# Order of four pieces of work at the edges of the feed-forward products, and the sizes of two down parts

## Chip, cores and metric

The kernel runs on one core of one Trainium2 chip. The metric is the device time of one execution in microseconds (us). Beside it stands one profiled execution, from which all rows below are taken.

## What is computed

The reference applies two layers and then one block to a sequence of 1024 positions of width 1024, all in fp32:

```python
for layer in range(2):
    y = conv_lru_mixer(x, ...) if layer == 0 else diff_attention_mixer(x, ...)
    x = layer_norm(DN_ALPHA * x + y, mix_ln_g[layer], mix_ln_b[layer])
    x = layer_norm(DN_ALPHA * x + swiglu(x, w_gate, w_up, w_down), ffn_ln_g[layer], ffn_ln_b[layer])
...
c_mod = silu(c) @ w_ada + b_ada            # six rows: sh1, sc1, g1, sh2, sc2, g2
...                                        # mLSTM and Fourier mixer of block 2
h2 = ln_plain(x) * (1 + sc2) + sh2
ff = square(relu(h2 @ w_ff1 + b_ff1)) @ w_ff2 + b_ff2
out = ln_affine(ALPHA * x + (1 + g2) * ff, ln2_g, ln2_b)
```

`swiglu(x, g, u, d)` is `(silu(x @ g) * (x @ u)) @ d`, with 2816 inner columns (22 tiles of 128); block 2 has 4096 (32 tiles).

## The kernel before

Every fp32 operand is split into a high part (a copy rounded to the matmul's format, made by ScalarE, L213) and a low part (the difference, made by VectorE, L214). A product then takes three matmuls, high by high (L235), high by low (L236) and low by high (L237). A weight tile arrives in a slot of the pool `raw` (three slots of 4 KB a partition, issued by SyncE at L218) and is split into `wh` and `wl`, or into the pair `wd`.

The sequence stands in 8 token blocks of 128. The three stretches of feed-forward work (layers 0 and 1, block 2) each have two stages.

**Up stage.** `run_ffn` goes over units, each a 2 by 2 block product by Winograd's scheme with seven products instead of eight: `prepare` loads two raw weight tiles, splits A11 and A12, and forms the sums S1 to S4 with four VectorE instructions (L674 to L677). `product` runs seven terms of 12 matmuls (128x128 by 128x512): A11·B11 and A12·B21 on `wx` (`corner`, `corner2`), T2, T3 and T4 on `wy`, T1 and B22 on `wz`. Between them stand small instructions: `keep` (L693, ScalarE) is a copy of A11·B11, `wy += keep` (L707, VectorE), a copy `u` of `wy` (L709, ScalarE), a copy `p` of `wz` (L713), `wz += u` (L714), and the sum for block 22 (L758, inside `sum22`), which must be done before T4 goes on with `wy`. The results are written to memory (`hd`).

The activations' blocks T1 to T3 and the sums of them (`bs`, `bl`) are formed by `xn.sums` on VectorE, once per pair of token blocks. Before the last sums exist, the products of the corner alone can run; `start` issues some of these early units (table `EARLY`) while the mixer before it ends. This overlap of a mixer's last token blocks with the first units is called a front here: one each in layer 0, layer 1 and block 2. The stage tables of `pipe` give the order in which `more` (it calls `start`) and `xn.sums` are issued.

**Down stage.** The inner tiles are cut into parts (`PARTS1`, `PARTS2`), each a number of inner tiles and the pool in which its split weights lie. A part goes over the 8 token blocks; `tokens` loads the activated tiles of a block back (`ht`, L831, in pieces of at most four inner tiles) and splits them, `down_tile` multiplies them (6 matmuls for each inner tile), and `add` adds the result to `xr` (L898). In the last part the token blocks also go through the layer norm and the first products of what follows (`stages`; `pv` are value projections), one behind another. While layer 1 goes through its parts, a side stream loads the 48 tiles of `w_ada` (two per token block), which VectorE multiplies and sums (L1240).

The text is written in program order, but a list scheduler turns it into the order in which each engine runs its instructions; every engine then works strictly in that order, and so does SyncE's queue of transfers.

Of the kernel before, what the change touches and what calls it, by code (L numbers as in the profile page):

```python
# [30 lines left out]
PARTS1 = ((8, "x"), (6, "u"), (4, "x"), (4, "u"))  # L31
# [129 lines left out]
class Net:  # L161
# [248 lines left out]
    def mixer_even(self, xr, xn, start):  # L410
# [220 lines left out]
        for c in range(NC1, 4):  # L631
# [3 lines left out]
                         (LE + ME[2], more), (LE + 1, norm), (LE + 2, feat), (LE + 3, xn.sums), (LE + 3, more)],  # L635
# [64 lines left out]
    def product(self, o, x, keep, finish, sum22, early):  # L700
# [13 lines left out]
        nc.vector.tensor_add(pz, pz, u2)  # L714
        self.term(py, o["S3"], x, "T3", False, True)
        sum22(py, p5)
        if not early:
            self.corner2(o, x, px, finish)
# [5 lines left out]
    def run_ffn(self, nf, x, src, nm, done, parts, down_weight, load, add, stages, side=None, add_half=None):  # L724
# [67 lines left out]
        o = prep(0)  # L792
        while begun:
            finish_first()
        for n, (q, m) in enumerate(order):
            nxt = prep(n + 1) if n + 1 < len(order) else None
            finish, sum22 = finisher(q, m)
            self.product(o, x, keep(q, m), finish, sum22, (q, m) in started)
            if m == nm - 1:
                ctx.pop(q)  # L800
            if n % 2:
                kept.pop(n // 2)
            o = nxt
            steps(SD[n % 2])

# [14 lines left out]

        def tokens(j, i):
            n, hs = parts[j][0], []
            for a in range(0, n, 4):
                e = min(n, a + 4)
                shape = (P, 2, e - a, P)
                if add_half is None and j == len(parts) - 1:
                    t = self.u("ht", shape, F32R)
                else:
                    t = self.wp.tile(list(shape), F32R, tag="w", name=self.name("ht"))
                raw = t[:, 1].bitcast(F32)  # L830
                nc.sync.dma_start(raw, hd[j][a:e, :, blk(i)].rearrange("f p t -> p f t"))  # L831
                self.split(t[:, 0], t[:, 1], raw)
                hs += [(t[:, 0, b, :], t[:, 1, b, :]) for b in range(e - a)]
# [3 lines left out]
        ws, hs = {0: weights(0)}, {}  # L837
# [139 lines left out]
    def mixer_odd(self, x, xr, xn, start):  # L977
# [218 lines left out]
        for _ in last:  # L1196
# [6 lines left out]
                   (LO + MO[1], more), (LO + MO[2], more), (LO + 3, sums), (LO + 3, more)])  # L1203
# [122 lines left out]
    def block2_mix(self, x, xr, xn, start):  # L1326
# [480 lines left out]
        def more(i):  # L1807
            if i == NTT - 1:
# [4 lines left out]
                  + [(LM, feat), (0, moments), (LM + 1, lambda i: xn.sums(i) if i >= 4 else None), (LM + 1, more)])  # L1813

    def block2_ff(self, x, xr, out):
# [15 lines left out]
        def load(i):  # L1831
            if i == 0:
# [3 lines left out]
                nc.gpsimd.tensor_mul(st["b2"], st["b2"], st["g2"])  # L1836
# [3 lines left out]
        def add(i, p, first, last):  # L1840
            nc.vector.scalar_tensor_tensor(xr[i], xr[i], ALPHA2 if first else 1.0, p, op0=ALU.mult, op1=ALU.add,
                                           accum_out=self.sum_of(xr[i]) if last and S4 else None)
            if cnt[i] == 1:
                nc.gpsimd.tensor_add(xr[i], xr[i], st["b2"])
# [180 lines left out]
```

## Time and profile before

| | |
|---|---|
| time, median of 3 runs | 3423.69 us (3421.68 to 3425.16) |
| profiled execution, its own time | 3421.3 us |
| its span | 3419.5 us |
| TensorE (PE) busy | 3269.5 us, 96% of the span |
| VectorE (DVE) busy | 2185.5 us, 64% |
| ScalarE (ACT) busy | 1412.9 us, 41% |
| GpSimd (POOL) busy | 265.6 us, 8% |
| mean granted clock of TensorE | 0.985 of full speed |

The span runs from the first to the last instruction; the execution's own time is 1.8 us longer. A time in the rows counts from the span's start. Matmuls are pipelined, so that one lasts longer than the distance to the next, and what counts for TensorE is the idle time in brackets ahead of an instruction with the instruction that ended it, and the clock that was granted.

### The profile page before, as it was taken

The page shows a single profiled execution, that of the slowest core. Times are in us where ns is not written, and L with a number is a line of the kernel's source. Part 1 is how long each engine was busy: PE and PEld are TensorE (multiplying, and loading weights), DVE is VectorE, ACT ScalarE, POOL GpSimd, SP SyncE. Part 2 cuts the span into 40 slices and gives each one's busy share as a digit, 9 for nine tenths or more (in the row PEclk, how much of TensorE's full clock was granted, in tenths as well). Part 3 has the DMA queues.
Part 4 walks back from the last instruction along what each step waited for, and adds up shares of the span by engine and source line. Part 5 has one row for each costly group of instructions (what it writes and reads, how often), then busy time and mean ns, then how long its engine had stood idle before and what let it go on. Part 6 is the DMA issues. An engine that isn't in the chain of part 4 may idle for free.

```text
span 3419.5 us, 40944 instructions
## 1 busy us (share of the span) xinstructions
PE 3269.5 (96%) x15588; PEld 2692.5 (79%) x15588; DVE 2185.5 (64%) x3445; ACT 1412.9 (41%) x2422; POOL 265.6 (8%) x458
## 2 busy tenths in 40 slices
PE   8998999999999999989999999999999989999998
PEld 7776788878877878877788878778777878878887
DVE  8997755555357677676765558654446876566635
ACT  4455433332237667655533332224334554432211
POOL 1011000000020111101000000013001300000201
PEclk9999999999999999999999999999999999999999
DMA  3131322235312111141332238721123333344312
GB/s 126 42 112 62 101 91 74 91 128 169 106 62 71 36 50 50 43 149 56 109 107 99 93 120 290 237 74 47 59 84 106 116 117 117 116 161 165 113 51 79
DMA packets 191764, 348.68 MB, mean 102 GB/s; under 512 B 14384, under 2 KB 105936, under 8 KB 191568
## 3 DMA queue, kind: packets, MB, share of 16 engines
q1 hardware_dynamic: 191568, 346.07, 30.6%
q8 instruction: 122, 2.00, 0.2%
q14 instruction: 74, 0.61, 0.1%
HBM read 268.41 MB, written 72.36 MB: 100 GB/s over the span
## 4 chain that ended last, share of the span: by engine, by line
PE 66%; DVE 13%; ACT 9%; DMA 5%; issue 4%; POOL 3%; SPq 0%; POOLq 0%; DVEq 0%; ACTq 0%
PE dn L236 6%; PE dn L235 6%; PE dn L237 6%; PE wy L235 4%; PE wy L236 4%; PE wy L237 4%; PE wx L235 3%; PE wx L237 3%; PE wx L236 3%; PE pi L235 3%; PE pi L236 3%; PE pi L237 2%; PE wz L235 2%; PE wz L237 2%; PE wz L236 2%
## 5 line engine op out<-in xcount | busy, mean ns | idle before, releaser
L213 ACT CAST wh<-raw 128x1024 fp32r<-128x1024 f32 (+1 forms) x275 | 282.7, 1048 | 405.1 <-DVE raw L677 138.1
L214 DVE TENSOR_TENSOR wl<-raw,wh 128x1024 fp32r<-128x1024 f32 (+1 forms) x275 | 334.3, 1233 | 132.1 <-ACT wh L213 128.1
L213 ACT CAST ht<-ht 128x512 fp32r<-128x512 f32 (+1 forms) x168 | 97.2, 580 | 448.0 <-DMA ht<-hd 438.7
L235 PE MATMUL dn<-wd,ht 128*128 128x512 f32 x704 | 274.4, 391 | 3.3 <-ACT wd L213 3.3
L236 PE MATMUL dn<-wd,ht 128*128 128x512 f32 x704 | 274.8, 390 | 1.3 <-DVE wd L214 1.2
L237 PE MATMUL dn<-wd,ht 128*128 128x512 f32 x704 | 274.4, 390 | 0.0
L235 PE MATMUL dn<-wh,ht 128*128 128x512 f32 x512 | 200.9, 392 | 10.8 <-DVE xr L898 6.7
L214 DVE TENSOR_TENSOR ht<-ht 128x512 fp32r<-128x512 f32 (+1 forms) x168 | 112.3, 673 | 153.2 <-ACT ht L213 152.4
L235 PE MATMUL wx<-bh,wh 128*128 128x512 f32 x480 | 192.2, 400 | 10.6 <-ACT keep L693 4.2
L237 PE MATMUL wx<-bh,wl 128*128 128x512 f32 x480 | 190.2, 397 | 11.2 <-DVE wl L214 11.2
L237 PE MATMUL dn<-wh,ht 128*128 128x512 f32 x512 | 200.3, 391 | 0.4 <-DVE ht L214 0.4
L236 PE MATMUL dn<-wl,ht 128*128 128x512 f32 x512 | 200.2, 391 | 0.0
L236 PE MATMUL wx<-bl,wh 128*128 128x512 f32 x480 | 190.3, 396 | 0.0
L235 PE MATMUL pi<-xh,wh 128*128 128x512 f32 x416 | 168.8, 406 | 7.8 <-DVE xl L214 7.8
L486 DVE SCALAR_TENSOR_TENSOR co<-ga,col,co 128x512 f32<-128x512 f32 (+18 forms) x240 | 165.4, 737 | 0.5
L237 PE MATMUL pi<-xh,wl 128*128 128x512 f32 x416 | 165.0, 397 | 0.0
L236 PE MATMUL pi<-xl,wh 128*128 128x512 f32 x416 | 164.9, 396 | 0.0
L235 PEld LDWEIGHTS dn<-wd,ht 128*128 128x128 f32 x704 | 132.3, 188 | 32.0 <-ACT wd L213 4.6
L236 PEld LDWEIGHTS dn<-wd,ht 128*128 128x128 f32 x704 | 132.4, 188 | 30.3 <-DVE wd L214 2.9
L237 PEld LDWEIGHTS dn<-wd,ht 128*128 128x128 f32 x704 | 132.4, 188 | 27.5
L287 POOL TENSOR_SCALAR nm<-sum 128x1 f32<-128x1 f32 x47 | 15.1, 322 | 1562.8 <-DVE xr L898 1323.1
L898 DVE SCALAR_TENSOR_TENSOR xr<-xr,dn 128x1024 f32<-128x1024 f32 x64 | 77.8, 1216 | 85.5 <-PE dn L237 81.3
(458 smaller groups left out, 8446.4 us busy)
## 6 DMA issues: line engine op xcount, KB each, us to landing
raw<-w_gu SPq DMA_DIRECT2D x100, 512.0 KB
hd<-g SPq DMA_DIRECT2D x152, 256.0 KB
raw<-w_f SPq DMA_DIRECT2D x70, 512.0 KB
ht<-hd SPq DMA_DIRECT2D x136, 256.0 KB
raw<-w_ada SPq DMA_DIRECT2D x48, 512.0 KB
raw<-w_dn SPq DMA_DIRECT2D x44, 512.0 KB
raw<-w_in SPq DMA_DIRECT2D x26, 512.0 KB
raw<-w_out SPq DMA_DIRECT2D x24, 512.0 KB
```

The source lines that it names most:

```text
L213: self.nc.scalar.copy(hi, src)
L214: (self.nc.gpsimd if pool else self.nc.vector).tensor_sub(lo, src, hi.bitcast(F32))
L235: mm(out, l[0], r[0], start=first, stop=False, **kw)
L236: mm(out, l[0], r[1], start=False, stop=False, **kw)
L237: mm(out, l[1], r[0], start=False, stop=last, **kw)
L287: (nc.vector if NMV else nc.gpsimd).tensor_scalar(nm, a, -1.0 / D, None, op0=ALU.mult)
L486: nc.vector.scalar_tensor_tensor(co[c][:, a:hi_], ga[c][:, a - s:hi_ - s], self.c("conv_w", 31 * c + 30 - s), co[c][:, a:hi_], op0=ALU.mul ...
L898: nc.vector.scalar_tensor_tensor(xr[i], xr[i], DN_ALPHA if first else 1.0, p, op0=ALU.mult, op1=ALU.add, accum_out=self.sum_of(xr[i]) if l ...
```

## The change

1. In layers 0 and 1 the parts of the down product change from 8, 6, 4, 4 inner tiles to 8, 4, 4, 6. The last part, of six, takes its `ht` tiles from the pool `raw` instead of the pool `u`.
2. In `product`, A12·B21 runs ahead of T3 instead of behind it.
3. The weights of the first down part are issued ahead of the last unit's product instead of behind it.
4. At the three fronts the last `more` (early units) is issued ahead of the last `xn.sums`.
5. In block 2 the bias row `b2` is scaled, and added to the 8 token blocks, by VectorE instead of GpSimd.

```diff
--- before.py
+++ after.py
@@ -28,7 +28,7 @@
 NF2 = 4096 // P
 NEG = -1.0e30
 EARLY, WAHEAD = (1, 1, 2, 2), 2
-PARTS1 = ((8, "x"), (6, "u"), (4, "x"), (4, "u"))
+PARTS1 = ((8, "x"), (4, "u"), (4, "x"), (6, "u"))
 PARTS2 = ((8, "x"), (6, "u"), (8, "x"), (6, "u"), (4, "x"))
 L2 = 2
 DV = 1
@@ -632,7 +632,7 @@
             conv(c, 1)
         more = lambda i: start() if i == NTT - 1 else None
         self.pipe(pre + [(0, lambda i: feat(i - 4)), (LE, prod_a), (LE + ME[0], more), (LE + ME[1], more),
-                         (LE + ME[2], more), (LE + 1, norm), (LE + 2, feat), (LE + 3, xn.sums), (LE + 3, more)],
+                         (LE + ME[2], more), (LE + 1, norm), (LE + 2, feat), (LE + 3, more), (LE + 3, xn.sums)],
                   range(4, 8))
 
     def mixer_end(self, xr, xn, layer):
@@ -712,10 +712,10 @@
         p5 = self.tmp("p5")
         nc.scalar.copy(p5, pz)
         nc.vector.tensor_add(pz, pz, u2)
+        if not early:
+            self.corner2(o, x, px, finish)
         self.term(py, o["S3"], x, "T3", False, True)
         sum22(py, p5)
-        if not early:
-            self.corner2(o, x, px, finish)
         self.term(pz, o["S4"], x, "B22", False, True)
         finish(0, 1, pz)
         self.term(py, o["A22"], x, "T4", False, True)
@@ -788,20 +788,6 @@
         def prep(n):
             q, m = order[n]
             return self.prepare(src(2 * q, m), src(2 * q + 1, m), first=(q, m) not in started)
-
-        o = prep(0)
-        while begun:
-            finish_first()
-        for n, (q, m) in enumerate(order):
-            nxt = prep(n + 1) if n + 1 < len(order) else None
-            finish, sum22 = finisher(q, m)
-            self.product(o, x, keep(q, m), finish, sum22, (q, m) in started)
-            if m == nm - 1:
-                ctx.pop(q)
-            if n % 2:
-                kept.pop(n // 2)
-            o = nxt
-            steps(SD[n % 2])
 
         def weights(j):
             n, kind = parts[j]
@@ -818,13 +804,30 @@
                 ws.append((t[:, e, :], t[:, e + 1, :]))
             return ws
 
+        ws = {}
+        o = prep(0)
+        while begun:
+            finish_first()
+        for n, (q, m) in enumerate(order):
+            nxt = prep(n + 1) if n + 1 < len(order) else None
+            finish, sum22 = finisher(q, m)
+            if nxt is None:
+                ws[0] = weights(0)
+            self.product(o, x, keep(q, m), finish, sum22, (q, m) in started)
+            if m == nm - 1:
+                ctx.pop(q)
+            if n % 2:
+                kept.pop(n // 2)
+            o = nxt
+            steps(SD[n % 2])
+
         def tokens(j, i):
             n, hs = parts[j][0], []
             for a in range(0, n, 4):
                 e = min(n, a + 4)
                 shape = (P, 2, e - a, P)
                 if add_half is None and j == len(parts) - 1:
-                    t = self.u("ht", shape, F32R)
+                    t = self.rp.tile(list(shape), F32R, tag="raw", name=self.name("ht"))
                 else:
                     t = self.wp.tile(list(shape), F32R, tag="w", name=self.name("ht"))
                 raw = t[:, 1].bitcast(F32)
@@ -834,7 +837,7 @@
             return hs
 
         todo = [(j, i) for j in range(len(parts)) for i in range(NTT)]
-        ws, hs = {0: weights(0)}, {}
+        hs = {}
 
         def ahead(n):
             if n < len(todo) and todo[n] not in hs:
@@ -1200,7 +1203,7 @@
         more = lambda i: start() if i == NTT - 1 else None
         sums = lambda i: xn.sums(i) if i >= 4 else None
         self.pipe([(0, lambda i: heads4(i, 4)), (LO + MO[0], more), (LO + 2, feat), (LO + 1, norm), (LO, o_prod),
-                   (LO + MO[1], more), (LO + MO[2], more), (LO + 3, sums), (LO + 3, more)])
+                   (LO + MO[1], more), (LO + MO[2], more), (LO + 3, more), (LO + 3, sums)])
 
     def ada(self):
         nc, A = self.nc, self.A
@@ -1810,7 +1813,7 @@
 
         stats = lambda i: self.ln_stats(xr[i])
         self.pipe([(3, stats), (4, stats), (1, prep), (3, norm1), (4, norm2), (2, prod)] + [(m, more) for m in MF]
-                  + [(LM, feat), (0, moments), (LM + 1, lambda i: xn.sums(i) if i >= 4 else None), (LM + 1, more)])
+                  + [(LM, feat), (0, moments), (LM + 1, more), (LM + 1, lambda i: xn.sums(i) if i >= 4 else None)])
 
     def block2_ff(self, x, xr, out):
         nc, A = self.nc, self.A
@@ -1833,7 +1836,7 @@
                 st["b2"] = self.u("b2")
                 r12 = ROWS.index("b_ff2")
                 nc.sync.dma_start(st["b2"], A["rows"][r12:r12 + 1, :].to_broadcast([P, D]))
-                nc.gpsimd.tensor_mul(st["b2"], st["b2"], st["g2"])
+                nc.vector.tensor_mul(st["b2"], st["b2"], st["g2"])
             xr.append(self.u("xr"))
             nc.sync.dma_start(xr[i], self.xs[2][blk(i), :])
 
@@ -1841,7 +1844,7 @@
             nc.vector.scalar_tensor_tensor(xr[i], xr[i], ALPHA2 if first else 1.0, p, op0=ALU.mult, op1=ALU.add,
                                            accum_out=self.sum_of(xr[i]) if last and S4 else None)
             if cnt[i] == 1:
-                nc.gpsimd.tensor_add(xr[i], xr[i], st["b2"])
+                nc.vector.tensor_add(xr[i], xr[i], st["b2"])
             cnt[i] += 1
 
         def add_half(i, p, cs):
```

The numbers of matmuls and their sizes stay. How the order on the engines changes is seen at three places. A line number behind the edit is 3 higher in the changed kernel (L887 is L890, L971 is L974), and the number at the end of a tile's name counts tiles and differs between the two.

**VectorE at the front of layer 0.** `wl_2714` is the low part of the weights of the early unit that TensorE waits for, in the changed kernel `wl_2698`; `ts`, `bs` and `bl` (L150 to L153, L214) are the sums, and the last `bl_2448` closes them. Before:

```order
L153 TENSOR_TENSOR ts_2661<-f_2229,ts_2660 128x512
L887 TENSOR_TENSOR g_2619<-g_2619,wx_2593 128x512
L214 TENSOR_TENSOR bl_2448<-ts_2660,bh_2447 128x8x128
L214 TENSOR_TENSOR bs_2453<-ts_2661,bs_2451 128x2x128
L214 TENSOR_TENSOR bs_2454<-ts_2661,bs_2452 128x2x128
L214 TENSOR_TENSOR bs_2461<-ts_2661,bs_2459 128x2x128
L214 TENSOR_TENSOR bs_2462<-ts_2661,bs_2460 128x2x128
L214 TENSOR_TENSOR wl_2714<-raw_2711,wh_2713 128x1024
L214 TENSOR_TENSOR w_390_2755<-raw_2753,w_390_2755 128x512
L674 TENSOR_TENSOR raw_2753<-raw_2753 128x512
L675 TENSOR_TENSOR raw_2753<-raw_2751,raw_2753 128x512
L676 TENSOR_TENSOR raw_2751<-raw_2753,raw_2751 128x512
```

In the changed kernel `wl` is found among the sums of the pair before the last:

```order
L150 TENSOR_TENSOR ts_2644<-f_2523,f_2154 128x512
L152 TENSOR_TENSOR ts_2645<-f_2523 128x512
L151 TENSOR_TENSOR ts_2644<-f_2523,ts_2644 128x512
L214 TENSOR_TENSOR wl_2698<-raw_2695,wh_2697 128x1024
L214 TENSOR_TENSOR bs_2352<-f_2631,bs_2350 128x2x128
L214 TENSOR_TENSOR bs_2353<-f_2631,bs_2351 128x2x128
L153 TENSOR_TENSOR ts_2645<-f_2154,ts_2644 128x512
L214 TENSOR_TENSOR bl_2448<-ts_2644,bh_2447 128x8x128
```

And the last sums are found some ten rows further on:

```order
L676 TENSOR_TENSOR raw_2751<-raw_2753,raw_2751 128x512
L677 TENSOR_TENSOR raw_2751<-raw_2751 128x512
L150 TENSOR_TENSOR ts_2729<-f_2631,f_2229 128x512
L152 TENSOR_TENSOR ts_2730<-f_2631 128x512
L151 TENSOR_TENSOR ts_2729<-f_2631,ts_2729 128x512
L214 TENSOR_TENSOR wl_2763<-raw_2751,wh_2762 128x1024
L153 TENSOR_TENSOR ts_2730<-f_2229,ts_2729 128x512
L214 TENSOR_TENSOR bl_2448<-ts_2729,bh_2447 128x8x128
L214 TENSOR_TENSOR bs_2453<-ts_2730,bs_2451 128x2x128
L214 TENSOR_TENSOR bs_2454<-ts_2730,bs_2452 128x2x128
```

`wl` moved from behind the sums of the last pair to the middle of the sums of the pair before it, and the sums of the weights (L674 to L677) moved ahead of the last sums, which now end with `bl_2448` behind `wl_2763`.

**VectorE at the last unit of layer 0.** `xr` is the residual's first scaling (L894 and L895, L897 and L898 in the changed kernel), `wd` the weights of the first down part. Before:

```order
L214 TENSOR_TENSOR ht_5375<-ht_5375 128x512
L894 TENSOR_TENSOR xr_5449<-xr_5449,gb_5383 128x1024
L707 TENSOR_TENSOR wy_5242<-wy_5242,keep_5126 128x512
L895 TENSOR_TENSOR xr_5449<-xr_5449,gb_5385 128x1024
L214 TENSOR_TENSOR wd_5333<-raw_5331,wd_5333 128x1024
L714 TENSOR_TENSOR wz_5258<-wz_5258,u_702_5256 128x512
L214 TENSOR_TENSOR wd_5333<-raw_5336,wd_5333 128x1024
L758 TENSOR_TENSOR p_704_5271<-wy_5242,p_704_5271 128x512
L214 TENSOR_TENSOR wd_5342<-raw_5340,wd_5342 128x1024
L887 TENSOR_TENSOR g_5185<-g_5185,p_704_5271 128x512
```

In the changed kernel:

```order
L897 TENSOR_TENSOR xr_5449<-xr_5449,gb_5383 128x1024
L214 TENSOR_TENSOR ht_5375<-ht_5375 128x512
L898 TENSOR_TENSOR xr_5449<-xr_5449,gb_5385 128x1024
L707 TENSOR_TENSOR wy_5278<-wy_5278,keep_5126 128x512
L214 TENSOR_TENSOR wd_5230<-raw_5228,wd_5230 128x1024
L214 TENSOR_TENSOR wd_5230<-raw_5233,wd_5230 128x1024
L214 TENSOR_TENSOR wd_5239<-raw_5237,wd_5239 128x1024
L714 TENSOR_TENSOR wz_5294<-wz_5294,u_714_5292 128x512
L890 TENSOR_TENSOR g_5185<-g_5185,wx_5264 128x512
L758 TENSOR_TENSOR p_716_5307<-wy_5278,p_716_5307 128x512
```

`wy += keep` (L707) moved behind both instructions on `xr_5449`, and three `wd` stand ahead of `wz += u` (L714) instead of one.

**SyncE's queue in the last down part of layer 0.** `ht` are the activated tiles (of the part `hd_95`), `raw<-w_v` the value weights for the `pv` products of layer 1's mixer, `spill` the layer's result written to memory. Before, where `w_v` had been issued long ahead of this part:

```order
L831 DMA ht_6711<-hd_95 128x4x128
L971 DMA spill<-xr_5387 128x1024
L831 DMA ht_6775<-hd_95 128x4x128
L971 DMA spill<-xr_5449 128x1024
L831 DMA ht_6894<-hd_95 128x4x128
L971 DMA spill<-xr_5547 128x1024
L831 DMA ht_6985<-hd_95 128x4x128
L971 DMA spill<-xr_5609 128x1024
L971 DMA spill<-xr_5671 128x1024
```

In the changed kernel:

```order
L834 DMA ht_6715<-hd_95 128x4x128
L974 DMA spill<-xr_5449 128x1024
L834 DMA ht_6719<-hd_95 128x2x128
L218 DMA raw_6776<-w_v 128x1024
L974 DMA spill<-xr_5535 128x1024
L218 DMA raw_6782<-w_v 128x1024
L834 DMA ht_6850<-hd_95 128x4x128
L834 DMA ht_6854<-hd_95 128x2x128
L834 DMA ht_6957<-hd_95 128x4x128
L974 DMA spill<-xr_5597 128x1024
L834 DMA ht_6961<-hd_95 128x2x128
```

Each token block now has two `ht` tiles, both in `raw` slots, and the two `w_v` tiles stand between the `ht` tiles of the sixth block and those of the seventh.

## Rows read from the trace of the kernel before

**Rows 1.** The page, part 1: busy time of each engine.

```profile
PE 3269.5 (96%) x15588; PEld 2692.5 (79%) x15588; DVE 2185.5 (64%) x3445; ACT 1412.9 (41%) x2422; POOL 265.6 (8%) x458
```

**Rows 2.** Waits of PE: total us, times, longest us, by line and releaser.

```profile
PE wx L237 <- DVE wl L214: 11.2, 3, 4.5
...
PE dn L235 <- DVE xr L898: 6.7, 5, 2.8
...
PE wy L235 <- ACT u L709: 5.7, 5, 2.1
```

**Rows 3.** Windows: us, then busy us (instructions) of PE, PEld, DVE, ACT, POOL; clock; DMA.

```profile
365.34:372.82 7.48, 6.80 (x22) 4.99 (x23) 5.23 (x7) 2.48 (x3) 0.00 (x0) 0.77 0.21 70
...
480.00:580.00 100.00, 100.00 (x440) 82.17 (x439) 56.89 (x72) 32.76 (x45) 0.00 (x0) 1.00 0.25 85
...
1658.48:1667.38 8.90, 8.22 (x22) 6.03 (x23) 5.67 (x7) 2.48 (x3) 0.00 (x0) 0.62 0.41 123
```

**Rows 4.** Timeline, layer 0 front: start, us, instruction, [idle before <-releaser].

```profile
361.59 1.22 DVE L214 TENSOR_TENSOR bl<-ts,bh 128x1024 fp32r<-128x1024 f32 x1
...
364.07 1.21 DVE L214 TENSOR_TENSOR wl<-raw,wh 128x1024 fp32r<-128x1024 f32 x1
...
365.34 0.50 PE L237 MATMUL wx<-bh,wl 128*128 128x512 f32 x1 [3.82 <-DVE wl L214]
```

**Rows 5.** Timeline of PE at the fronts of layer 1 and block 2.

```profile
1658.48 0.50 PE L237 MATMUL wx<-bh,wl 128*128 128x512 f32 x1 [2.91 <-DVE wl L214]
...
2768.80 0.53 PE L237 MATMUL wx<-bh,wl 128*128 128x512 f32 x1 [4.52 <-DVE wl L214]
```

**Rows 6.** Timeline, last unit of layer 0.

```profile
753.88 0.69 DVE L707 TENSOR_TENSOR wy<-wy,keep 128x512 f32<-128x512 f32 x1
...
755.24 0.50 PE L235 MATMUL wy<-bs,wh 128*128 128x512 f32 x1 [1.85 <-ACT u L709]
```

**Rows 7.** Timeline, start of the down product of block 2.

```profile
3054.35 0.50 PE L235 MATMUL dn<-wd,ht 128*128 128x512 f32 x1 [2.49 <-ACT wd L213]
...
3054.66 5.67 DVE L214 TENSOR_TENSOR wd<-raw,wd 128x1024 fp32r<-128x1024 f32 x3
...
3055.16 2.95 POOL L1836 TENSOR_TENSOR b<-b,mrow 128x1024 f32<-128x1024 f32 x1 [313.54 <-DMA b<-rows]
```

**Rows 8.** Timeline, last token blocks of layer 0.

```profile
1020.08 0.47 PE L235 MATMUL dn<-wh,ht 128*128 128x512 f32 x1 [1.53 <-DVE xr L898]
...
1025.41 0.39 PE L237 MATMUL dn<-wh,ht 128*128 128x512 f32 x1
...
1029.33 1.21 DVE L898 SCALAR_TENSOR_TENSOR xr<-xr,dn 128x1024 f32<-128x1024 f32 x1
...
1038.94 0.58 PE L235 MATMUL pv<-wh,xh 128*128 128x256 f32 x1 [4.26 <-ACT xh L213]
```

**Rows 9.** Timeline, last token blocks of layer 1.

```profile
2294.36 0.54 PE L235 MATMUL dn<-wh,ht 128*128 128x512 f32 x1 [4.13 <-ACT ht L213]
...
2321.24 0.39 PE L237 MATMUL dn<-wh,ht 128*128 128x512 f32 x1
...
2325.19 1.21 DVE L898 SCALAR_TENSOR_TENSOR xr<-xr,dn 128x1024 f32<-128x1024 f32 x1
...
2336.37 0.79 PE L235 MATMUL pi<-xh,wh 128*128 128x512 f32 x1 [7.84 <-DVE xl L214]
```

**Rows 10.** Timeline of SP and ACT: one ht tile issued and landed.

```profile
3055.18 0.39 SPq L831 DMA_DIRECT2D ht<-hd  x1
...
3057.56 0.62 ACT L213 CAST ht<-ht 128x512 fp32r<-128x512 f32 x1 [1.37 <-DMA ht<-hd]
```

**Rows 11.** Timeline, the stream of w_ada tiles beside the down product of layer 1.

```profile
2188.70 1.23 DVE L1240 SCALAR_TENSOR_TENSOR raw<-raw,cact 128x1024 f32<-128x1024 f32 x1 [2.40 <-DMA raw<-w_ada]
...
2191.22 0.47 PE L235 MATMUL dn<-wh,ht 128*128 128x512 f32 x1 [2.75 <-DVE xr L898]
```

**Rows 12.** Timeline of DVE, a unit in the middle of layer 0.

```profile
507.65 0.69 DVE L758 TENSOR_TENSOR g<-wy,p 128x512 f32<-128x512 f32 x1 [1.89 <-PE wy L237]
```

## Prediction

> **What bounds the kernel now.** I read the page first: TensorE is busy 96% of the span [rows 1], so about 150 us without a matmul is all that a new order can win, the matmuls being the same. In a steady unit 440 matmuls of 512 columns start in 100 us, 0.227 us apart, at full clock [rows 3]; twelve (one term) take 2.7 us. Next the waits of TensorE, to see which idle time the edits can touch: a low weight part in the early units, the residual's sum in the down products, the copy `u` at the end of the units [rows 2]. Last the timelines at these places. A wait has a second price: after the wait of 3.82 us at the front of layer 0 the next 22 matmuls took 7.48 us at a granted clock of 0.77, after the one in layer 1 8.90 us at 0.62 [rows 3]. At full clock 22 take 5.0. The lower level (1.2 GHz, for part of the stretch) costs one minus the granted clock, times the stretch: 1.7 and 3.4 us.
>
> **The change part by part.** *Front of layer 0 (early units ahead of the last sums).* TensorE waits 3.82 us for one `wl`, which VectorE reaches at 364.07, straight behind the last sums [rows 4]. Now that `wl` stands before them, so the 22 matmuls start at 361.5 and end at 366.5. But the last sums pay: ahead of the final `bl_2448` there now stand two `wl` (1.21 each) and five half-size instructions on the weights (0.69 each), 5.9 us in all. Before, it ended at 362.8 [rows 4]; now about 368.7. TensorE waits there for 2.4 us and starts the T term at 368.9 instead of 372.82: 3.9 us won, or 2.2 if the clock falls after the new wait. I take **-3** (-2.2 to -3.9).
>
> *Front of layer 1.* The same places. The wait began 2.91 us before 1658.48 [rows 5] and the T term started at 1667.38, 11.8 us later. Now 5.0 for the 22 matmuls and, as above, a wait of some 2.4, 7.4 in all: 4.4 won. **-4** (-3 to -5).
>
> *Front of block 2.* The wait of 4.52 [rows 5] is for a `wl` of the same kind, but here the last sums come out ahead of the weights' sums, so that the next `wl` is late by nearly as much. The wait moves: **-0.5** (-1.2 to 0).
>
> *End of the units, layers 0 and 1 (A12·B21 ahead of T3, `wd` forward).* T3 waits 1.85 us for `u`, because `wy += keep` starts at 753.88 between two residual instructions [rows 6]. A12·B21 now fills 2.7 us there, and though L707 slips behind the second of them to about 755.0, T3 would start at 756.3, 0.2 late. What is late next: three casts of `wd` on ScalarE stand ahead of the copy `p`, and three differences (1.22 each) on VectorE ahead of L714, which ends about 761.2. T3 ends at 759.0, so B22 waits some 2.2 us. In place of 1.85 the layer pays 2.4, and with what the down product then finds I take **+1 for each layer, +2** (from -2, if the casts are early, to +6, if the clock falls each time).
>
> *Start of the down product of block 2.* TensorE waits 2.49 us for the first `wd`, then VectorE takes 5.67 us for three differences of 1.22 [rows 7]: 2.0 too many, while GpSimd's `b2` multiplication of 2.95 us runs. The change puts the first three `wd` into the last unit and takes that GpSimd instruction away: **-4.5** (-2, as the eighth tile can still be late, to -6.5, with the clock).
>
> *`b2` on VectorE.* One instruction here and eight at the token blocks behind it move over, 9 times 1.22, 11 us of VectorE. What hides them is the down product of 32 inner tiles with VectorE mostly idle. Cost 0; without that cover 11. The Trainium skill (Perfetto Trace Analysis, Optimizing Scalar/DVE Operations) says that work may be taken off a saturated VectorE to GpSimd, but that the two share a read port, so that it might not help. The first half speaks against the edit and would give +11, the second for it. The trace agrees with the second: the three differences were stretched by 2.0 us.
>
> *Last part of six tiles, layer 0.* In the last part a token block had 24 matmuls of the down product, and behind them the block's norm, transposes and value products; TensorE waited four times for `xr` of the block before, 6.7 less 2.75 (layer 1, [rows 11]), 3.95 us in all [rows 2], 1.53 at most [rows 8]. Twelve more matmuls a block, taken from an earlier part that has no idle time, cover these: -3.95. The end of the chain too: the last `dn` ends at 1025.6, but L898 of that block starts at 1029.33 behind the late chain of the block before, and the last wait is 4.26 [rows 8]. With 2.7 us more of TensorE per block the chain is on time: up to -3.7. Against it a new wait. The `ht` tiles and the two `w_v` tiles now share three slots: the second `w_v` can be issued only after 24 matmuls of the sixth block. Landing of a tile half its size takes 2.4 us [rows 10], the cast about 1 (0.62 for half the size, [rows 10]) and the difference 1.2, so 5 to 6 us against 3 to 4 us of other matmuls: +2 (0 to 5). Sum **-5.5** (-1 to -8).
>
> *The same in layer 1.* The wait of 4.13 [rows 9] ends with the `ht` cast, queued on ScalarE behind the norm of an earlier block; with 36 matmuls a block it should be covered, and a lowered clock of some 1.7 with it. The last `dn` ends at 2321.5, its L898 starts at 2325.19, 3.7 late, and 7.84 is waited at the end [rows 9]; -3.7 there. The value weights in the slots again +2. Sum **-7.5** (-3 to -11).
>
> *The side stream.* In layer 1 VectorE waits 2.40 us for a `w_ada` tile, L898 queues behind it, and TensorE waits 2.75 [rows 11]. The second part now has 24 matmuls a block, 5.4 us instead of 8.2, with the same two tiles of `w_ada` each. I keep the old wait and add one like it: **+3** (0 to +6).
>
> *Steady units.* A12·B21 ahead of T3 moves no wait that the trace shows. But L758 must now be done within the 12 matmuls of B22, where it had 24. It starts when T3 is done and takes 0.69 [rows 12]; of 2.7 us 2.0 are spare, 0.8 with one `wl` ahead. Cost 0.
>
> The sum is -3 - 4 - 0.5 + 2 - 4.5 - 5.5 - 7.5 + 3 = -20. The profiled execution took 3421.3, 2.4 below the median 3423.7; 3421.3 - 20 = 3401.3, and so a median of **3403.7**.
>
> **Rivals.** *The waits only move.* The fronts give nothing, as I expect of block 2, and the tails half, because chain and slots are as tight as before: 2 - 4.5 - 6.5 + 3 = -6, 3418. For it: at each place I already found the next late instruction. Against: TensorE's work per block and its 22 matmuls do become ready earlier.
>
> *Slower: the slots of `raw`.* Each block takes two of three slots in both last parts, so the first `ht` of the block after next is issued only when this block's `dn` is done; SyncE is in order, and a `spill` or `w_v` that waits holds `ht` behind it. Against it: 2.4 of landing, 0.62 and 0.69 to split, 3.7 in all, fit into the 8.2 us of a block's 36 matmuls. It decides from 20/16 = 1.25 us lost per block on 16 blocks; at 2.5 the sum is +20, 3444.
>
> *Slower: L758 late in steady units.* With two `wl` ahead of it T4 waits 0.4 us. There are 42 such units (22, 22 and 16, less six early ones each); 0.5 each eats the gain, and 1 us each gives +22, 3446. VectorE stands idle 1.89 us ahead of L758 [rows 12], which speaks against it.
>
> *More.* Both end waits vanish and their lowered clock too: about -32, 3392.
>
> **How the numbers follow.** The measurement tells 0.2% (6.8 us) from no change: the three runs span 3.5. Forecast 0.68, by itself 3394 to 3414 (the half-widths of the terms, 0.9, 1, 0.6, 4, 2.2, 3.5, 4 and 3, added as squares, give 8; I take 10). Waits only move 0.17, slots 0.08, L758 0.03, more 0.04. Faster is the forecast, more, and the third of "only move" that falls below 3416.8: 0.77. Same 0.12, slower 0.11. The range 3391 to 3425 takes in "more" in part and all of "only move".
>
> **What would show it.** Right: no wait over 2.5 us for `wl` at L237 at the fronts of layers 0 and 1, but one of about 2.4 ahead of `wy`; at 3054 a wait under 1 us; in the last parts `dn` no longer waits for `xr`, and the end waits are 1 and 4 us instead of 4.26 and 7.84. Wrong: `dn` waits ended by `ht` with a transfer behind it, block after block; waits of `wy` at L758 in the units; more waits behind L1240.

## The result and the profile after

The changed kernel took 3384.09 us (median of 4 runs, 3382.54 to 3388.97), against 3423.4 us before (4 runs); the ratio is 0.9888, 95% interval 0.987 to 0.9905. That is 38 us less (0.0112 of 3423.4), about twice the 20 that were forecast, and below the range of 3391 to 3425. Run again later beside other kernels it took 3389.84 us (ratio 0.9896, 0.9882 to 0.991): 35 us less.

The chip's record of the clock and the page's first part give the first split of the gain, which is to be compared with [rows 1] and the clock of 0.985 before:

```profile
core 0: 3380.8 us, clock 0.990
...
PE 3251.6 (96%) x15588; PEld 2685.3 (79%) x15588; DVE 2179.8 (64%) x3454; ACT 1413.9 (42%) x2422; POOL 242.9 (7%) x449
```

The busy time of TensorE fell by 17.9 us with the same matmuls, since at the lower clock they last longer; span times one minus the clock falls from 51 us (0.015 x 3419.5) to 34, by 17. The rest of the 39 us that the profiled span lost, some 21, is idle time. Nearly half of the gain is clock; some 3 of its 17 us lie in stretches that no edit touches (before, 0.83 over 20 us from 195 and from 2525 us; after, 0.91 at the same places).

The waits of TensorE after (us in total, times, longest) answer to [rows 2]:

```profile
PE dn L235 <- DVE xr L901: 6.8, 6, 2.4
...
PE wz L235 <- DVE wz L714: 3.5, 5, 1.4
...
PE wy L235 <- ACT u L709: 2.2, 3, 1.0
```

The wait for `wl` at L237 (11.2 us in three) is gone from the list, that for `u` fell from 5.7 to 2.2, and that at L714 rose from 0.2 to 3.5. The wait of `dn` for the residual is as large as before, but in six pieces, none over 2.4.

Where the time went is best read by position in TensorE's stream: both kernels run 15588 matmuls and transposes, and at the borders of the stages the same ones have been done. The differences of the time between borders, in us, for the two profiled executions of the changed kernel ("changed", and "again" for the later one) against the one of before, and the forecast's terms:

| stretch | forecast | changed | again |
|---|---|---|---|
| front of layer 0 | -3 | -4.8 | -4.7 |
| front of layer 1 | -4 | -4.8 | -4.6 |
| front of block 2 | -0.5 | -1.6 | -1.1 |
| units of layer 0, layer 1, block 2 | 0 | -1.5, -2.2, -1.3 | -1.8, -2.4, -0.2 |
| last units of layers 0 and 1 | +2 | -1.0, -0.7 | -1.7, -1.3 |
| start of the down product, block 2 | -4.5 | -6.4 | -5.0 |
| last part, layer 0 | -5.5 | -2.5 | -3.7 |
| last part, layer 1 | -7.5 | -8.6 | -9.6 |
| earlier parts of layer 1 (side stream) | +3 | +0.4 | +2.4 |
| stretches that no edit touches | 0 | -3.6 | +1.1 |
| sum | -20 | -39 | -33 |

The stretches that no edit touches differ by up to some 3 us from one execution to another, in both directions; a single number of this table is good to 1 or 2 us where transfers take part, and to 0.3 in the units of layers 0 and 1; those of block 2 differ by 1.1.

**A wait that the list of waits doesn't show.** In the middle of layer 0, where the forecast had put 0, every second unit of the kernel before holds this (timeline before; start, us, instruction; ScalarE first, then TensorE):

```profile
619.12 0.59 ACT L709 COPY u<-wy 128x512 f32<-128x512 f32 x1 [1.61 <-DVE wy L707]
...
619.38 0.39 PE L235 MATMUL wx<-bh,wh 128*128 128x512 f32 x1
...
619.75 0.50 PE L235 MATMUL wy<-bs,wh 128*128 128x512 f32 x1
...
620.10 0.40 PE L236 MATMUL wy<-bs,wh 128*128 128x512 f32 x1
```

The first matmul of T3 starts 0.37 us after the matmul before it (the fourth of A12·B21, which the scheduler had already put between), not 0.227, lasts 0.50 instead of 0.39, and the next follows 0.35 later: some 0.3 us lost with the slower starts behind it, with no bracket, and no row in the list. It is the wait for `u` in small: the copy ends at 619.71, T3 starts at 619.75; four matmuls between T1 and T3 don't cover it, twelve do. In the changed kernel T1 runs into A12·B21 at the usual distance, and T3 behind it too:

```profile
611.94 0.39 PE L237 MATMUL wz<-bh,wl 128*128 128x512 f32 x1
...
612.17 0.39 PE L235 MATMUL wx<-bh,wh 128*128 128x512 f32 x1
...
614.66 0.39 PE L237 MATMUL wx<-bh,wl 128*128 128x512 f32 x1
...
614.89 0.39 PE L235 MATMUL wy<-bs,wh 128*128 128x512 f32 x1
```

The 16, 16 and 10 steady units have 21 pairs. The trace before has 21 such starts of T3 behind `wx`, 0.35 to 0.37 us apart, and the changed kernel none. 21 times 0.3 is over 6; 5.0 and 4.4 were measured.

**The fronts.** TensorE's wait for `wl` became short waits for other operands (the first two at the front of layer 0, then one in layer 1; windows: us, busy us, granted clock, DMA share, GB/s):

```profile
365.52 0.51 PE L235 MATMUL wy<-bh,wh 128*128 128x512 f32 x1 [0.46 <-ACT bh L213]
...
366.47 0.50 PE L235 MATMUL wz<-bh,wh 128*128 128x512 f32 x1 [0.44 <-ACT wh L213]
...
1648.68 0.49 PE L235 MATMUL wy<-bh,wh 128*128 128x512 f32 x1 [0.41 <-ACT bh L213]
...
365.00:392.00 27.00, 25.72 (x110) 1.00 0.36 111
...
1638.00:1672.00 34.00, 33.14 (x142) 1.00 0.29 93
```

The waits ahead of `wy` are 0.46 and 0.41 instead of 2.4, with a second of 0.44 and 0.45 ahead of `wz` behind each. By the starts the front of layer 0 still loses 1.7 us here: from 364.67 to 367.54 five distances take 2.87 us, where 1.14 would do. The clock stays at 1.00, where it fell to 0.77 and 0.62 [rows 3]. VectorE did run as replayed:

```profile
353.15 1.22 DVE L214 TENSOR_TENSOR wl<-raw,wh 128x1024 fp32r<-128x1024 f32 x1
...
365.69 1.22 DVE L214 TENSOR_TENSOR bl<-ts,bh 128x1024 fp32r<-128x1024 f32 x1
```

`wl` stands 12.5 us ahead of the last `bl`. But the T term starts with the high part (`wy<-bh`), which ScalarE makes, and needs `bl`, which I took for its start, only for the matmuls that follow; the scheduler put `wz<-bh` between. In block 2 the wait moved, as forecast, though to a `wh` and not to the next `wl` (timeline; [rows 5] before):

```profile
2744.76 0.50 PE L235 MATMUL wy<-bh,wh 128*128 128x512 f32 x1 [2.95 <-ACT wh L213]
```

**Last units.** The wait of 1.85 for `u` [rows 6] became one of 0.86 at L714, behind three `wd`:

```profile
745.45 0.69 DVE L707 TENSOR_TENSOR wy<-wy,keep 128x512 f32<-128x512 f32 x1
...
747.75 3.50 DVE L214 TENSOR_TENSOR wd<-raw,wd 128x1024 fp32r<-128x1024 f32 x3 [1.60 <-ACT wd L213]
...
751.16 0.69 DVE L714 TENSOR_TENSOR wz<-wz,u 128x512 f32<-128x512 f32 x1
...
751.91 0.50 PE L235 MATMUL wz<-bs,wh 128*128 128x512 f32 x1 [0.86 <-DVE wz L714]
```

This is the order that the forecast replayed, and VectorE's part of it was right: from the start of L707 to the end of L714 6.4 us, where I had 6.2. But L707 starts just as T1 ends and A12·B21 begins, and I had it 1.6 us later, behind residual blocks that now had come in earlier; so T3 waits for nothing, and B22 0.86 instead of 2.2.

**Start of the down product of block 2.** One wait of 0.6 us is left, at the eighth tile, and TensorE's clock doesn't fall there (in the later execution three waits, 1.7 us in all, at a clock of 1.00):

```profile
3017.00:3052.00 35.00, 34.41 (x151) 1.00 0.83 276
...
3028.47 1.22 DVE L1839 TENSOR_TENSOR b<-b,mrow 128x1024 f32<-128x1024 f32 x1
```

The multiplication by `b2` takes VectorE 1.22 us, between two `wd`.

**Last part, layer 0.** The idle time is larger than the forecast's new wait of 2:

```profile
PE dn L235 <- DVE xr L901: 3.5, 3, 2.4
...
PE pv L235 <- ACT wh L213: 2.4, 2, 2.0
...
PE dn L235 <- ACT f L342: 1.0, 1, 1.0
...
986.64 0.33 SPq L218 DMA_DIRECT2D raw<-w_v  x1
...
992.34 1.04 ACT L213 CAST wh<-raw 128x1024 fp32r<-128x1024 f32 x1 [6.98 <-DMA raw<-w_v]
...
979.39 0.79 PE L235 MATMUL dn<-wh,ht 128*128 128x512 f32 x1 [2.38 <-DVE xr L901]
...
993.44 0.39 PE L235 MATMUL pv<-wh,xh 128*128 128x256 f32 x1 [1.97 <-ACT wh L213]
```

The second `w_v` tile is issued at 986.64, when its slot is free, and ScalarE waits 6.98 us for it with the `ht` casts and the norms queued behind; VectorE too. TensorE's waits for `w_v` are 2.4 us, about the forecast's 2. The rest is something else: of the four waits for `xr` [rows 2] some are back, 3.5 us in all. The one of 2.38 stands ahead of the second `w_v`: L901 runs there behind a difference `xl`, for which VectorE had waited 4.85 us. The end wait of 4.26 [rows 8] is gone.

**Last part, layer 1.** The 4.13 is gone, and the last L898 (now L901) is on time, waiting for TensorE itself:

```profile
2297.02 1.22 DVE L901 SCALAR_TENSOR_TENSOR xr<-xr,dn 128x1024 f32<-128x1024 f32 x1 [0.50 <-PE dn L237]
...
2308.45 0.79 PE L235 MATMUL pi<-xh,wh 128*128 128x512 f32 x1 [4.57 <-ACT wh L213]
...
2260.00:2322.00 62.00, 56.26 (x322) 0.94 0.31 106
```

The end wait is 4.57 instead of 7.84 [rows 9], and ends with the cast of a weight, not with `xl`.

### The profile page after: what moved, and what is told of

It reads as the page before. It is cut to its first block, busy times and chain, and to the rows that moved or that the text cites. A ratio compares the mean times of both kernels' runs of the same rounds, so it can differ in the third digit from the quotient of the medians.

```text
span 3380.8 us, 40966 instructions
## 1 busy us (share of the span) xinstructions
PE 3251.6 (96%) x15588; PEld 2685.3 (79%) x15588; DVE 2179.8 (64%) x3454; ACT 1413.9 (42%) x2422; POOL 242.9 (7%) x449
## 4 chain that ended last, share of the span: by engine, by line
PE 68%; DVE 12%; ACT 8%; DMA 5%; issue 3%; POOL 2%; SPq 0%; DVEq 0%; POOLq 0%; ACTq 0%
PE dn L236 7%; PE dn L237 7%; PE dn L235 7%; PE wy L236 4%; PE wy L237 4%; PE wy L235 4%; PE wz L235 3%; PE wx L235 3%; PE pi L235 3%; PE pi L236 3%; PE wx L236 3%; PE wx L237 3%; PE wz L236 2%; PE wz L237 2%; PE pi L237 2%
## 5 line engine op out<-in xcount | busy, mean ns | idle before, releaser
L214 DVE TENSOR_TENSOR wl<-raw,wh 128x1024 fp32r<-128x1024 f32 (+1 forms) x275 | 329.9, 1218 | 121.7 <-ACT wh L213 117.7
L237 PE MATMUL dn<-wd,ht 128*128 128x512 f32 x704 | 273.9, 389 | 0.0
L214 DVE TENSOR_TENSOR ht<-ht 128x512 fp32r<-128x512 f32 (+1 forms) x168 | 106.9, 638 | 178.6 <-ACT ht L213 177.9
L237 PE MATMUL dn<-wh,ht 128*128 128x512 f32 x512 | 200.0, 391 | 0.1
L237 PE MATMUL wx<-bh,wl 128*128 128x512 f32 x480 | 187.4, 391 | 0.0
L237 PE MATMUL pi<-xh,wl 128*128 128x512 f32 x416 | 165.0, 397 | 0.0
L237 PEld LDWEIGHTS dn<-wd,ht 128*128 128x128 f32 x704 | 132.2, 188 | 27.3
L235 PEld LDWEIGHTS dn<-wh,ht 128*128 128x128 f32 x512 | 96.5, 188 | 29.0 <-issue 4.3
```

The lines of the kernel that those rows point to most:

```text
L214: (self.nc.gpsimd if pool else self.nc.vector).tensor_sub(lo, src, hi.bitcast(F32))
L235: mm(out, l[0], r[0], start=first, stop=False, **kw)
L237: mm(out, l[1], r[0], start=False, stop=last, **kw)
```

## The experiments

Each kernel was timed in 5 rounds beside the kernel before; where the verdict rests on a stretch, the position table is taken of its profile, against the same execution of before. The first four make one edit alone.

**Only A12·B21 moved** (edit 2, in `product`):

```diff
+        if not early:
+            self.corner2(o, x, px, finish)
         self.term(py, o["S3"], x, "T3", False, True)
         sum22(py, p5)
-        if not early:
-            self.corner2(o, x, px, finish)
```

> Only A12·B21 moved ahead of T3, all else as before. Theory of the recorded sum: the steady units give 0, only the waits of 1.85 and 2.08 us for u in the last units of layers 0 and 1 go, so about -3.5 us. Theory from the two traces (the waits for u recur in every second unit, too short for the list of waits): 0.3 us for each pair of units, -5.5 in the units, and with the waits in the last and first units -9 to -10 us.

Measured: 3417.03 us against 3425.23 of the kernel before, ratio 0.9974 (0.9963 to 0.9984), 9 us less. In the profile the last units give -2.2 and -2.0 and the steady units -1.3, -1.6 and -1.0. The theory from the traces holds: a re-ordering that I had costed at 0 in the units gives 4 us there, as much as in the two visible waits, and none of the 21 late starts of T3 is left in this run either.

**Only the parts** (edit 1):

```diff
-PARTS1 = ((8, "x"), (6, "u"), (4, "x"), (4, "u"))
+PARTS1 = ((8, "x"), (4, "u"), (4, "x"), (6, "u"))
...
-                    t = self.u("ht", shape, F32R)
+                    t = self.rp.tile(list(shape), F32R, tag="raw", name=self.name("ht"))
```

> Only the parts 8, 4, 4, 6 with the last part's ht in raw slots. Recorded sum: -5.5 in layer 0, -7.5 in layer 1, +3 by the side stream, -10 us. From the traces: -2.3 in layer 0 and -8.3 in layer 1 with the side stream, -10.6 us, with new waits of about 2 us for value weights in layer 0 only. The two agree on the sum and differ on layer 0 and on the side stream (a wait behind w_ada tiles of 3 us more, or none).

Measured: 3416.64 us, ratio 0.9968 (0.9955 to 0.998), 11 us less. Last part of layer 0 -2.9, of layer 1 -8.9, and the earlier parts of layer 1 +2.9. The profiled execution is only 3.6 us shorter than that of before, as stretches that this edit leaves alone are 5 us longer in it. The sum doesn't tell the two theories apart; the stretches say that layer 0 gives half of what was forecast. The side stream's price of +3 is not shown: in the four kernels with the old parts the same stretch differs from before by -2.7 to +5.5, in those with the new parts by -0.7 to +6.2.

**Only the fronts** (edit 4):

```diff
-                         (LE + 2, feat), (LE + 3, xn.sums), (LE + 3, more)],
+                         (LE + 2, feat), (LE + 3, more), (LE + 3, xn.sums)],
...
-                   (LO + 3, sums), (LO + 3, more)])
+                   (LO + 3, more), (LO + 3, sums)])
...
-                  + [(LM, feat), (0, moments), (LM + 1, lambda i: xn.sums(i) if i >= 4 else None), (LM + 1, more)])
+                  + [(LM, feat), (0, moments), (LM + 1, more), (LM + 1, lambda i: xn.sums(i) if i >= 4 else None)])
```

> Only the early units ahead of the last sums. Recorded sum: -3, -4 and -0.5 us at the three fronts, -7.5. From the traces: -4.0, -4.8 and -1.6, -10.4 us.

Measured: 3412.59 us, ratio 0.9958 (0.9945 to 0.9971), 14 us less, more than either theory. The profile shows -4.8, -4.6 and -0.1 at the three fronts, and its whole span is 10.0 shorter. Most of the remaining 4 us lies in the comparison: the profiled execution of before, 3421.3, is itself 3.9 below the median of 3425.23 in these rounds. In block 2 the wait only moves, as forecast.

**Only the first down weights forward** (edit 3; `b2` stays on GpSimd):

```diff
+            if nxt is None:
+                ws[0] = weights(0)
             self.product(o, x, keep(q, m), finish, sum22, (q, m) in started)
...
-        ws, hs = {0: weights(0)}, {}
+        hs = {}
```

> Only the first down weights ahead of the last unit's product; b2 stays on GpSimd. Recorded sum: the casts of wd stand ahead of the copy p and B22 waits, +1 us in each of layers 0 and 1 beside the waits for u that stay, and -2.5 to -4.5 in block 2: about -1.5 us. From the traces: nothing lost in layers 0 and 1, and -6.4 us in block 2, less what the GpSimd multiplication still costs: -4 to -6 us.

Measured: 3422.9 us, ratio 0.999 (0.9981 to 0.9998), 3 us less: between the two. The last units of layers 0 and 1 change by 0.0 and -0.3, the start of block 2's down product by -4.6. The theory of the sum is wrong on the layers, by 1 each, and right on block 2.

One minus each of the four ratios, times 3425, is 8.9, 11.0, 14.4 and 3.4 us, 37.7 in all, near the 35 and 38 of the changed kernel, which has `b2` on VectorE besides. Each ratio is good to some 4 us; within this the edits add up.

The next three take one edit out of the changed kernel.

**A12·B21 back behind T3.**

```diff
-        if not early:
-            self.corner2(o, x, px, finish)
         self.term(py, o["S3"], x, "T3", False, True)
         sum22(py, p5)
+        if not early:
+            self.corner2(o, x, px, finish)
```

> The changed kernel with A12·B21 put back behind T3. Theory that the re-ordered product gives about 9 us by short waits in the units: 9 us slower than the changed kernel, about 3393 us. Recorded sum: only the last units are touched, 3 us slower at most, about 3387.

Measured: 3398.43 us, ratio 0.9925 (0.9912 to 0.9938), 10 to 13 us above the changed kernel (0.9896 and 0.9888). This is a little more than the theory's 9. The late starts of T3 are back, 21 of them, and the last units of layers 0 and 1 now cost +2.0 and +1.8 against before, where A12·B21 in front of T3 had made it -1.0 and -0.7. In the last unit of layer 0 (timeline of TensorE, then a window):

```profile
750.94 0.59 PE L235 MATMUL wy<-bs,wh 128*128 128x512 f32 x1 [2.22 <-ACT u L709]
...
750.00:760.00 10.00, 9.06 (x33) 0.83 0.49 164
```

This is not the loss that I forecast for `wd` forward. The only wait is that for `u`, 2.22 where it was 1.85 (2.28 and 2.08 in layer 1), and behind it the clock falls, 1.7 us in each layer, which it didn't before (1.00 over 30 us); B22 doesn't wait for L714 at all. Nor does it with `wd` alone forward and the same old order (0.0 and -0.3): A12·B21, then between T3 and B22, covers `wd`. The forecast's wait of B22 needs both edits, and comes to 0.86 and 1.36 (0.15 and 0.75 in the later execution).

**The old parts.**

```diff
-PARTS1 = ((8, "x"), (4, "u"), (4, "x"), (6, "u"))
+PARTS1 = ((8, "x"), (6, "u"), (4, "x"), (4, "u"))
...
-                    t = self.rp.tile(list(shape), F32R, tag="raw", name=self.name("ht"))
+                    t = self.u("ht", shape, F32R)
```

> The changed kernel with the parts 8, 6, 4, 4 and the last ht tiles from the pool u. Both theories: the tails lose what the six-tile part gave, 10 us, about 3394. If the gain of the tails were due to the shift of all work by the other edits, the time would stay near 3384.

Measured: 3404.06 us, ratio 0.9937 (0.9925 to 0.9949), 14 to 17 us above the changed kernel, where 10 were expected. Last parts +0.6 and -0.3 against before: the tails' gain is the parts' and nothing else's. (The earlier parts of layer 1 cost +5.5 here.)

**`b2` back on GpSimd**, and beside it **only its multiplication**:

```diff
-                nc.vector.tensor_mul(st["b2"], st["b2"], st["g2"])
+                nc.gpsimd.tensor_mul(st["b2"], st["b2"], st["g2"])
...
-                nc.vector.tensor_add(xr[i], xr[i], st["b2"])
+                nc.gpsimd.tensor_add(xr[i], xr[i], st["b2"])
```

> The changed kernel with the b2 multiplication and the eight additions back on GpSimd. Theory of the recorded sum: the additions cost nothing on either engine, the multiplication costs up to 2 us by stretching the wd differences, if these still lie beside it: 3384 to 3386 us. Rival, that VectorE stretched eight times more holds up the down product: 3390 or more.

> The changed kernel with only the b2 multiplication back on GpSimd, the eight additions on VectorE. If the multiplication alone stretches a VectorE instruction ahead of the last wd, this loses what the whole of b2 on GpSimd lost at the down start, 5 us there, about 3388 to 3389. Rival, that the additions cost it: 3384 to 3385.

Measured: 3388.18 us, ratio 0.9894 (0.9881 to 0.9907), and with the multiplication alone 3386.98, ratio 0.9888 (0.9874 to 0.9902). The intervals overlap those of the changed kernel (0.9888 and 0.9896), and the times don't settle it; the profiles say something of the place. The start of the down product wins 1.3 and 3.8 us against before, the changed kernel 6.4 and 5.0. With `b2` on GpSimd (timeline of VectorE and GpSimd, then a window of TensorE's clock):

```profile
3023.74 2.87 POOL L1839 TENSOR_TENSOR b<-b,mrow 128x1024 f32<-128x1024 f32 x1 [312.53 <-DMA b<-rows]
...
3024.27 2.89 DVE L1825 TENSOR_TENSOR g<-g 128x512 f32<-128x512 f32 x1
...
3027.09 1.21 DVE L214 TENSOR_TENSOR wd<-raw,wd 128x1024 fp32r<-128x1024 f32 x1
...
3027.00:3047.00 20.00, 17.80 (x62) 0.83 0.69 232
```

A squaring of half size, 0.69 us elsewhere, lasts 2.89 (2.88 with the multiplication alone), until 0.5 us behind the end of GpSimd's multiplication, and the `wd` difference behind it is 2.2 us late. TensorE waits three times, 2.2 us in all, and the clock falls (0.83 of 20 us, 3.4 us). With the multiplication alone on GpSimd it waits four times, 2.7 us, and the clock stays at 1.00. So the multiplication costs 1 to 3 us, of which the lower end is no more than the two executions of the changed kernel differ by (1.4), and the clock, if it falls, the rest; the eight additions show no wait of TensorE in either profile.

**Where the `ht` tiles lie.** The changed kernel with these tiles in the pool `u`, and with only the larger of a block's two there:

```diff
-                    t = self.rp.tile(list(shape), F32R, tag="raw", name=self.name("ht"))
+                    t = self.u("ht", shape, F32R)
...
-                if add_half is None and j == len(parts) - 1:
+                if add_half is None and j == len(parts) - 1 and e - a == 4:
+                    t = self.u("ht", shape, F32R)
+                elif add_half is None and j == len(parts) - 1:
                     t = self.rp.tile(list(shape), F32R, tag="raw", name=self.name("ht"))
```

> The changed kernel with parts 8, 4, 4, 6, but the ht tiles of the last part from the pool u (27 buffers) instead of the three raw slots. Theory that the slots cost a wait for value weights: 2 us in layer 0 (waits 2.38 and 1.97 in the trace) go, 3 to 4 us faster, about 3380. Rival, that the pool u is held longer by others: no change or slower by waits for ht.

> The changed kernel with the larger ht tile of each block in the pool u and the smaller one in a raw slot. If the value weights waited for slots, one slot per block instead of two sets most of the 8 us in the last part of layer 0 free: layer 0's waits of 2.38, 1.97 and 0.96 go, about 3378 to 3380. Rival, that any sharing holds SyncE's queue: 3383 to 3385.

Measured: in `u`, 3379.38 us, ratio 0.9866 (0.9854 to 0.9879); with the smaller tile in `raw`, 3385.13, ratio 0.9882 (0.9867 to 0.9896). By its total the second is no different from the changed kernel, as its rival said. The last part of layer 0 wins 11.3 us with none in `raw`, 6.5 with one tile of a block and 2.5 or 3.7 with both. With none, both `w_v` tiles are issued some 120 us earlier, the stretch that had 7 us of waits has these (all that the list of waits of TensorE has there), and the clock stays at 1.00:

```profile
855.88 2.54 SPq L218 DMA_DIRECT2D raw<-w_v  x2
...
PE dn L235 <- DVE xr L901: 0.6, 2, 0.4
...
937.00:1031.00 94.00, 93.35 (x522) 1.00 0.24 83
```

So the six-tile part covers what the forecast said it would, and more (-11.3 where I had -7.6 before the slots' price), and having the tiles in the slots takes 8 us of it back, where I had put 2. How the slots lead to the waits for `xr` no run shows; the order of VectorE's and ScalarE's instructions differs between the two kernels too. In layer 1 nothing of the kind shows: last part -11.2 there, but +3.8 in the earlier parts.

**A version faster than both.** With the `ht` tiles in `u` and the first down weights forward in block 2 alone:

```diff
-            if nxt is None:
+            if nxt is None and add_half is not None:
                 ws[0] = weights(0)
...
+        if 0 not in ws:
+            ws[0] = weights(0)
...
-                    t = self.rp.tile(list(shape), F32R, tag="raw", name=self.name("ht"))
+                    t = self.u("ht", shape, F32R)
```

> The changed kernel with the last part's ht tiles in the pool u and, in layers 0 and 1 only, the first down weights behind the last unit's product again. If the wd forward costs about 1 us in each of the two last units (with it these units won 1.0 and 1.0 us, A12·B21 alone 2.2 and 2.7), this is 2 to 3 us faster than the kernel with ht in u alone: about 3377. Rival, that the down product then waits for wd: 3379 to 3383.

> The changed kernel itself beside the others on the same chip: 3384 us. By both theories its ratio lies above those of the two kernels with ht in u by 0.002.

Measured on one chip: 3373.71 us, ratio 0.9851 (0.9837 to 0.9865), beside 3389.84, ratio 0.9896, of the changed kernel. Its last units give -2.2 and -2.0 with no wait at B22, the changed kernel's -1.0 and -0.7 or -1.7 and -1.3: `wd` forward costs 0.5 to 1.3 us in each here, and with `ht` in `u` nothing in layer 1 (-2.1). Against the kernel with the `ht` tiles in `u` alone the intervals overlap.

## Why the prediction was wrong

The direction held, and so did most of the mechanisms; the sum was about half the gain, and the time lies below the range. By its steps:

1. *"A12·B21 ahead of T3 moves no wait that the trace shows. ... Cost 0"* is the step that failed. The trace showed it, but not in the list of waits: in every second unit T3 started 0.37 us behind the matmul before it. Worth -5.0 and -4.4 by the two executions, and with the next point 9 of the 19 and 13 us that they gained beyond the sum. Moving A12·B21 alone (-1.3, -1.6, -1.0) shows it.
2. *End of the units, +2*, had the wrong sign: -1.7 and -3.0. The cost of `wd` forward was right in kind, as B22 waits at L714 behind three `wd`, but mis-sized: in layer 0 T3 waits for nothing, where the replay had 0.2, and B22 0.86, not 2.2, since L707 starts 1.6 us earlier than the replay had it.
3. *The fronts of layers 0 and 1, -3 and -4*: -4.8 and -4.8, then -4.7 and -4.6. The wait that I put at the T term, 2.4 us, is 0.46 and 0.41 with a second as short, because the term starts on the high part alone; and the clock doesn't fall there.
4. *The clock.* I charged it at the fronts and for one wait in layer 1, some 7 us. The lower clock also left the stretches at the front and the down start of block 2 and at the parts of layer 1 (0.97 to 1.00 in 60 us around the side stream, 0.90 to 0.94 in the last part). In all it gave back 17 of 39 us, out of TensorE's busy time. So the 150 us without a matmul are not all that a new order can win, as the prediction says at its start.
5. *Last part of layer 0, -5.5*, was too much: -2.5 and -3.7. The wait for `w_v` itself is 2.4, as forecast (+2), but with `ht` in the slots come waits for `xr` (3.5), one for `f` (1.0) and the clock (0.84 over 11 us, 1.8), some 8 in all. *Start of the down product, -4.5*: -6.4 and -5.0, within its bounds. *Last part of layer 1, -7.5*: -8.6 and -9.6, right. *Side stream, +3*: +0.4 and +2.4, within its bounds, but kernels with the old parts vary as much there, so no run shows this term.

Of the rivals, the slots of `raw` do cost (8 us in layer 0, in three or four waits and not block after block), but not enough to decide; L758 held T4 once, 0.36 us, in block 2; "the waits only move" happened in block 2 alone; "more" came nearest in the number (3392), but not by its mechanism: it had both end waits gone, and that of layer 1 is still 4.57. My errors, but for the last part of layer 0, were of one sign. A likely reason, which no run tests, is that each replay went on to the next late instruction at full price, while the short waits, and most of the clock that the old waits cost, were left out of the account.

## What to carry to other kernels

Where a kernel repeats a stretch many times, read one period's start-to-start distances of the busiest engine, not only the list of its waits: 0.3 us every 38 us has no bracket, and twenty of them are worth more than a visible wait. Count the clock at every wait that a change removes, and look in the trace after whether a new wait brings it back. When tiles are moved into a small pool, list what else goes through it in the same stretch: here activations and two weight tiles in three slots cost 8 of the 11 us that the larger part had won.

## What the runs showed of the hardware

A wait's length alone didn't tell whether TensorE's clock falls. Two windows of the changed kernel begin with the waits shown above, 2.38 us ahead of `dn` and 2.95 ahead of `wy`; the last two rows are the second place again, in the later execution of the same kernel:

```profile
979.00:990.00 11.00, 10.16 (x43) 0.84 0.28 100
...
2744.00:2754.00 10.00, 9.02 (x38) 1.00 0.46 131
...
2746.63 0.50 PE L235 MATMUL wy<-bh,wh 128*128 128x512 f32 x1 [2.92 <-ACT wh L213]
...
2746.00:2756.00 10.00, 9.16 (x31) 0.83 0.44 131
```

The shorter one was followed by a stretch with the lower of the two levels in it (0.84 over 11 us, 1.8 us lost), the longer one by none. The later execution waits as long there, 2.92, and the lower level does follow (0.83 over 10 us): the same wait at the same place of the same kernel went either way. The wait of 2.49 at the down start of block 2 [rows 7] had been followed by the lower level too (0.86 over 12 us). What decides it no run here shows.

VectorE and GpSimd: beside GpSimd's 2.87 us multiplication of 128x1024 a VectorE instruction of 0.69 us lasted 2.89 and ended 0.5 us after it. The same multiplication on VectorE takes 1.22.
